# Alternating the two heads of a tile in two attention layers, and padding the tiles that the products read

## The chip, the cores and the metric

The kernel runs on one core of a Trainium2 chip (trn2). The metric is the device time of one launch in microseconds; the median of three runs is quoted. The engines are called as in the profile: PE multiplies matrices (PEld is its loading of weights), DVE, ACT and POOL work on vectors, SP issues most transfers. Every core has a large memory SBUF, which all engines read, and a small one, PSUM, in eight banks of 128 partitions by 512 fp32 numbers, into which PE writes.

## The reference, cut to what matters

Two transformer blocks of two layers each, one after the other, on 512 tokens of width 1024 (the first block puts 16 learned tokens ahead: T = 528). A layer is a mixer and a gated feed-forward network (FFN), each behind a normalization and added to its input. The mixers are: RG-LRU beside sliding-window attention, retention, gated DeltaNet, and attention over three dilated windows. The change touches the two attentions, whose cores are

```python
# first block, layer 0: 8 query heads in 2 groups, one key/value head a group, 64 wide
s = concat([einsum('bnhgqk', q, k_meta), einsum('bnhgqk', q, k_window)]) * 64 ** -0.5   # 16 + 256 keys
s = where(mask, s, NEG_INF)
p = softmax(concat([s, sink]))[..., :-1]
o = p[..., :16] @ v_meta + p[..., 16:] @ v_window
...
# second block, its second mixer: 8 heads of 64, three groups (window, step) = (128, 1), (512, 4), (2048, 16)
logits = where(valid, einsum('brnqhd,brnkhd->brnhqk', q, k) + bias, -inf)   # tokens gathered by step
o_g = einsum('brnhqk,brnkhd->brnqhd', p / l, v);  lse_g = m + log(l)
o = sum_g softmax_g(lse_g) * o_g
```

All is fp32.

## The kernel before, in words

`tile_kernel` (from L1396) runs eight stages, called layers 0 to 7: mixer and FFN in turn. Stages 0 to 2 work on 528 tokens, mostly as two halves of 264; stages 3 to 7 on 512.

**The products.** Every dense product goes through `mm3` (L151). An fp32 number is kept as a high and a low part in PE's faster format fp32r, and each 128x128 block of weights costs three matmuls: high weights by high tokens (L157), high by low (L158), low by high (L159). Such a group is called a triple here. Weights come as 430 transfers of 512 KB and are split on ACT (`whi`, L136) and DVE or POOL (`wlo`, L137). The tokens, PE's moving operand, lie in eight tiles `hhi` and eight `hlo` from `head` (L111), 528 numbers wide whatever the stage, and in `ahi`/`alo` from `act_tile` (L306), as wide as the stage has tokens. Tiles of a name lie one behind the other in SBUF. A tile of 528 numbers takes 2112 bytes, which is 8 x 256 + 64, so its next neighbour begins 64 bytes further on modulo 256; that remainder is called the place of a tile. The eight `hhi` tiles thus go twice through the places 192, 0, 64, 128, in the order in which a product takes them, while `ahi`/`alo` of the stages with 512 tokens (2048 bytes) all have one place, 64. The weights lie at 128.

**The attention of layer 0** (`layer_ab`). `scores(b, kv)` takes a block b of 128 queries and one key/value head kv: four products of 64 rows (the 64 numbers of a head lie on partitions 0 to 63 or 64 to 127), for b > 1 in two pieces of 16 and 256 keys (L565, L566), otherwise in one (L569), then softmax on DVE and ACT. `values(b, kv, s, po)` turns the probabilities round (transposes, L600), copies them out on ACT (L602) and multiplies them with the values (L603), whose result takes 64 of the bank's partitions.

**The attention of layer 6** (`layer_dsw`) goes by four pairs of heads. For each head of the pair: the scores of the undilated group (L1257) and of the two dilated ones (L1266), four to a bank, which DVE takes out of PSUM with scale and bias (`put`, L1249); later the transposes (L1333) and the products with the values (L1349, L1351, and L1363 for the dilated groups). The bias table `tb` of a pair is loaded and the mask added on POOL (L1197).

These products are in plain fp32, and PE does each as two passes, which the profile counts as two matmuls.

**The order** on each engine is set by a scheduler that simulates times and puts first what has priority: the attentions have it, in a strand "b" with its own PSUM banks (4 in layer 0, 3 in layer 6), and the dense products of the same stage fill in between. `aux()` gives the next bank of the strand.

Of the kernel before, what the change touches and what calls it, by code (L numbers as in the profile page):

```python
# [13 lines left out]
OP = mybir.AluOpType  # L14
# [8 lines left out]
HT = T // 2  # L23
NFF = 22
# [27 lines left out]
class Net:  # L52


    def __init__(self, ctx, tc, A):
# [5 lines left out]
        self.hp = ctx.enter_context(tc.tile_pool(name="head", bufs=1))  # L61
        self.hpp = ctx.enter_context(tc.tile_pool(name="headp", bufs=1, space=PSUM))
# [9 lines left out]
    def layer(self, name, acts, width, banks, tmp, pool_split=False):  # L72
# [160 lines left out]
    def rstd(self, sq, n, groups, mul, add):  # L233
# [6 lines left out]
        if G == 2:  # L240
            wide = self.tp.tile([128, 640], F32, name="wide", tag="wide" + self.cur, bufs=2)[:, :m * 64]
            nc.vector.tensor_copy(wide.rearrange("p (g c) -> p g c", c=64), col[:, :, None].to_broadcast([128, m, 64]))
# [62 lines left out]
    def act_tile(self):  # L305
        return (self.ap.tile([128, self.wact], F32R, name="ahi", tag="ahi", bufs=self.nact),  # L306
                self.ap.tile([128, self.wact], F32R, name="alo", tag="alo", bufs=self.nact))
# [133 lines left out]
def layer_ab(N, ctx):  # L441
# [14 lines left out]
    rope = pl.tile([128, 2, T], F32, name="rope")  # L456
# [7 lines left out]
    wa = pl.tile([128, 4, 128], F32, name="wa")  # L464
    nc.gpsimd.dma_start(wa, A["lru_wa"])
    wi = pl.tile([128, 4, 128], F32, name="wi")
# [49 lines left out]

    yah = pl.tile([128, 4, T], F32R, name="yah")
    yal = pl.tile([128, 4, T], F32R, name="yal")

    def attention():  # L520
# [35 lines left out]
        def scores(b, kv):  # L556
# [3 lines left out]
            r = kv * 64  # L560
            s = wk.tile([128, 4, 272], F32, name="s", bufs=3)
            for j in range(4):
                ps = N.aux()
                if b > 1:
                    nc.tensor.matmul(ps[:, 0:16], qkv[r:r + 64, 2 + j, q0:q0 + 128], k[r:r + 64, 0:16], start=True, stop=True)  # L565
                    nc.tensor.matmul(ps[:, 16:nk], qkv[r:r + 64, 2 + j, q0:q0 + 128], k[r:r + 64, q0 - 128:q0 + 128],  # L566
                                     start=True, stop=True)
                else:
                    nc.tensor.matmul(ps[:, :nk], qkv[r:r + 64, 2 + j, q0:q0 + 128], k[r:r + 64, 0:nk], start=True, stop=True)  # L569
                if b == 0:  # L570
# [1035 lines left out]
```

## Time and profile before

| | us |
|---|---|
| three runs | 2919.19, 2932.78, 2938.44 |
| median | 2932.78 |
| profiled execution | 2933.66 |
| its span | 2931.9 |
| PE busy | 2869.4 (98%) |
| DVE busy | 1498.4 (51%) |
| ACT busy | 1027.3 (35%) |
| POOL busy | 404.7 (14%) |

The span is what the profiler saw of the execution, from the first instruction to the last; the 1.8 us around it belong to the launch. Busy time of PE is the union of its matmuls, which overlap: a new one starts before the last has drained. What a matmul costs is therefore read from start to start, not from its duration. The mean clock granted to PE was 0.982 of 2.4 GHz.

### The profile page before, as it was taken

Reading aid. Unit: us, or ns where it says so; the run is one execution under the profiler, and the core shown is the slowest. Engines: PE = TensorE matmul, PEld = TensorE weight load, DVE = VectorE, ACT = ScalarE, POOL = GpSimd, SP = SyncE. Lnnn points to the kernel's source line nnn. Section 1 sums busy time; section 2 is a strip of 40 time slices with the busy share of each in tenths; the row PEclk is TensorE's granted clock in tenths of the full one; section 3 lists DMA queues with packets and bytes.
Section 4 is the critical chain, followed back from the end, with each engine's and each line's share of the span. In section 5 each row is a group of like instructions: output and inputs, shape, how many; then the busy total and the mean of one; then the engine's idle time right before and its main releaser. Section 6 shows DMA issues by size and latency. Waiting matters only on the chain.

```text
span 2931.9 us, 39986 instructions
## 1 busy us (share of the span) xinstructions
PE 2869.4 (98%) x16334; PEld 2455.0 (84%) x16334; DVE 1498.4 (51%) x2553; ACT 1027.3 (35%) x1735; POOL 404.7 (14%) x336
## 2 busy tenths in 40 slices
PE   7899999999999999999999899999999999999999
PEld 7768999998888888888878788888888877888887
DVE  6755953444455368834356854533335575533332
ACT  4634322332222233222266433422224555432221
POOL 3401201100000001001143443100003111000000
PEclk9879999999999999999999899999999999999999
DMA  4102942232212227722222111222222222122222
GB/s 147 54 29 97 340 146 94 94 109 87 72 66 72 87 80 280 258 94 94 91 93 65 58 66 65 94 93 94 94 94 93 75 75 68 51 94 94 95 99 73
DMA packets 93240, 294.79 MB, mean 101 GB/s; under 512 B 18736, under 2 KB 21168, under 8 KB 92928
## 3 DMA queue, kind: packets, MB, share of 16 engines
q1 hardware_dynamic: 91552, 288.59, 28.0%
q8 instruction: 128, 2.10, 0.3%
q10 hardware_dynamic: 1008, 2.22, 0.2%
q0 software_dynamic: 496, 1.43, 0.2%
q14 instruction: 56, 0.46, 0.0%
HBM read 287.42 MB, written 4.26 MB: 99 GB/s over the span
## 4 chain that ended last, share of the span: by engine, by line
PE 92%; DVE 4%; ACT 2%; POOL 1%; issue 1%; DMA 0%; SPq 0%; ACTq 0%; POOLq 0%; DVEq 0%
PE mm L157 26%; PE mm L159 26%; PE mm L158 26%; PE aux L770 1%; PE aux L603 1%; PE aux L227 1%; PE aux L157 1%; PE aux L158 1%; PE aux L159 1%; PE aux L762 1%; PE aux L250 1%; PE aux L1363 1%; PE aux L1333 1%; PE aux L1266 1%; DVE solve L1115 1%
## 5 line engine op out<-in xcount | busy, mean ns | idle before, releaser
L157 PE MATMUL mm<-hhi,whi 128*128 128x512 f32 (+2 forms) x3256 | 1116.3, 345 | 12.2 <-ACT whi L136 10.2
L158 PE MATMUL mm<-hlo,whi 128*128 128x512 f32 (+2 forms) x3256 | 1114.9, 343 | 3.5 <-DVE hlo L122 2.0
L159 PE MATMUL mm<-hhi,wlo 128*128 128x512 f32 (+2 forms) x3256 | 1116.7, 343 | 0.0
L136 ACT ACTIVATE whi<-wraw 128x1024 fp32r<-128x1024 f32 x430 | 455.8, 1061 | 1211.7 <-PE mm L158 849.4
L157 PEld LDWEIGHTS mm<-hhi,whi 128*128 128x128 f32 x3256 | 617.5, 190 | 83.4 <-ACT whi L136 10.2
L158 PEld LDWEIGHTS mm<-hlo,whi 128*128 128x128 f32 x3256 | 619.5, 190 | 76.4 <-DVE hlo L122 2.3
L137 DVE TENSOR_TENSOR wlo<-wraw,whi 128x1024 fp32r<-128x1024 f32 x388 | 485.2, 1251 | 382.4 <-ACT whi L136 381.0
L159 PEld LDWEIGHTS mm<-hhi,wlo 128*128 128x128 f32 x3256 | 619.5, 190 | 71.2 <-issue 0.6
L159 PE MATMUL mm<-ahi,wlo 128*128 128x512 f32 (+2 forms) x1079 | 375.4, 348 | 0.0
L158 PE MATMUL mm<-alo,whi 128*128 128x512 f32 (+2 forms) x1079 | 375.2, 348 | 0.0
L157 PE MATMUL mm<-ahi,whi 128*128 128x512 f32 (+2 forms) x1079 | 374.9, 349 | 0.1
L158 PEld LDWEIGHTS mm<-alo,whi 128*128 128x128 f32 x1079 | 203.2, 188 | 27.9 <-DVE alo L122 0.2
L157 PEld LDWEIGHTS mm<-ahi,whi 128*128 128x128 f32 x1079 | 202.8, 188 | 28.0 <-ACT ahi L121 0.6
L159 PEld LDWEIGHTS mm<-ahi,wlo 128*128 128x128 f32 x1079 | 202.8, 188 | 27.7 <-issue 0.2
L230 POOL TENSOR_TENSOR rcol<-rcol,mhalf 128x4 f32<-128x4 f32 (+4 forms) x46 | 60.0, 1306 | 1187.2 <-DVE rcol L229 1187.1
L388 DVE TENSOR_TENSOR t<-t,mm 128x512 f32<-128x512 f32 (+2 forms) x108 | 61.6, 570 | 210.3 <-PE mm L159 207.2
L380 POOL TENSOR_TENSOR t<-t,acc 128x264 f32<-128x264 f32 (+1 forms) x60 | 80.6, 1345 | 499.5 <-ACT t L379 499.5
L137 POOL TENSOR_TENSOR wlo<-wraw,whi 128x1024 fp32r<-128x1024 f32 x42 | 100.8, 2401 | 189.3 <-ACT whi L136 184.8
L419 DVE SCALAR_TENSOR_TENSOR araw<-araw 128x1024 f32<-128x1024 f32 x96 | 122.8, 1289 | 1.6 <-DMA araw<-in_w_ada 1.4
L432 DVE TENSOR_TENSOR X<-X,mm 128x264 f32<-128x264 f32 (+2 forms) x103 | 54.5, 529 | 115.3 <-PE mm L159 115.2
L121 ACT ACTIVATE ahi<-t 128x512 fp32r<-128x512 f32 (+2 forms) x128 | 69.6, 550 | 83.1 <-DVE t L388 58.3
L434 DVE SCALAR_TENSOR_TENSOR X<-mm,mod,X 128x512 f32<-128x512 f32 (+1 forms) x63 | 43.6, 698 | 93.5 <-PE mm L159 93.1
(459 smaller groups left out, 2739.7 us busy)
## 6 DMA issues: line engine op xcount, KB each, us to landing
wraw<-in_wstream SPq DMA_DIRECT2D x430, 512.0 KB, 3.2
araw<-in_w_ada SPq DMA_DIRECT2D x96, 512.0 KB, 5.3
tb<-in_dsw_bias SPq DMA_DIRECT2D x4, 640.0 KB, 4.6
X<-in_x SPq DMA_DIRECT2D x8, 264.0 KB, 10.8
xd<-X SPq DMA_DIRECT2D x1, 2048.0 KB, 9.1
X<-xd SPq DMA_DIRECT2D x1, 2048.0 KB, 8.5
out_dram<-X SPq DMA_DIRECT2D x4, 512.0 KB, 2.8
dec<-in_c_decay ACTq DMA_DIRECT2D x1, 1056.0 KB, 8.9
```

The costliest lines, as they stand in the source:

```text
L121: self.nc.scalar.activation(hi, src, AF.Copy)
L136: self.nc.scalar.activation(hi, src, AF.Copy)
L137: (self.nc.gpsimd if s < 2 else self.lo_eng).tensor_tensor(lo, src, hi.bitcast(F32), op=OP.subtract)
L157: mm(ps, wh, ah, start=start and k == 0, stop=False)
L158: mm(ps, wh, al, start=False, stop=False)
L159: mm(ps, wl, ah, start=False, stop=stop and k == n - 1)
L230: nc.gpsimd.tensor_tensor(col, col, self.mhalf[:, :m], op=OP.pow)
L380: nc.gpsimd.tensor_tensor(sg, sg, row[:, t0:t0 + n], op=OP.mult)
L388: nc.vector.tensor_mul(sg[:, :n], sg[:, :n], ps)
L419: nc.vector.scalar_tensor_tensor(r, r, 1.0, self.c, op0=OP.mult, op1=OP.mult, accum_out=self.mod[:, m:m + 1])
L432: nc.vector.tensor_add(x, x, ps)
L434: nc.vector.scalar_tensor_tensor(x, ps, gate_col[:, m:m + 1], x, op0=OP.mult, op1=OP.add)
```

## The change

Three things are changed. In layers 0 and 6 the loops are turned inside out: scores of both heads of a tile are issued in turn, each head into a bank of its own, and so are the products with the values, which go to the two halves of one bank. In `head` and `act_tile` tiles of 528 numbers become 576 wide (2304 bytes, 9 x 256), and a tile `pad` of 64 bytes, cleared by POOL, stands ahead of them: all `hhi`, `hlo`, `ahi`, `alo` then lie at place 192, the second half of the 528 tokens at 224. To make room, the mask of layer 6 shrinks (its middle part was a copy of its beginning), so that its add on POOL goes in four pieces a pair instead of one; some tiles of layer 0 share memory with others that are done (`rope`, `wa`, `wi`).

```diff
+TP = 576
...
+            if acts:
+                self.nc.gpsimd.memset(self.ap.tile([128, 16], F32, name="pad"), 0.0)
...
-        return tuple(self.hp.tile([128, T], F32R, name=n, tag=n, bufs=KD)[:, :self.wact] for n in ("hhi", "hlo"))
+        if not self.pad:
+            self.pad = self.hp.tile([128, 16], F32, name="pad")
+            self.nc.gpsimd.memset(self.pad, 0.0)
+        return tuple(self.hp.tile([128, TP], F32R, name=n, tag=n, bufs=KD)[:, :self.wact] for n in ("hhi", "hlo"))
...
+        w = S if self.wact == S else TP
+        return tuple(self.ap.tile([128, w], F32R, name=n, tag=n, bufs=self.nact)[:, :self.wact] for n in ("ahi", "alo"))
...
+    pts = [lambda tag=tag: pl.tile([128, 512], F32, name="pt", tag=tag) for tag in ("wa", "wi", "pt")]
...
+        def scores(b):
...
+            ss.append(pl.tile([128, 4, 272], F32, name="s", tag="rope") if b % 2 else wk.tile([128, 4, 272], F32, name="s", bufs=3))
             for j in range(4):
...
+                pss = [N.aux(), N.aux()]
+                parts = [(0, 16, 0), (16, nk, q0 - 128)] if b > 1 else [(0, nk, 0)]
+                for c0, c1, k0 in parts:
+                    for kv, r in enumerate(rows2):
+                        nc.tensor.matmul(pss[kv][:, c0:c1], qkv[r, 2 + j, q0:q0 + 128], k[r, k0:k0 + c1 - c0],
+                                         start=True, stop=True)
...
+                for s in ss:
+                    pt = N.aux()
+                    for j in range(4):
+                        nc.tensor.transpose(pt[:w, j * 128:j * 128 + 128], s[:, j, c:c + w], N.ident)
+                    p = pts[next(turn) % 3]()
+                    nc.scalar.activation(p[:w], pt[:w], AF.Copy)
+                    ps.append(p)
+                for r, p in zip(rows2, ps):
+                    nc.tensor.matmul(po[r], vt[:w, blk, r], p[:w], start=i == 0, stop=i == len(segs) - 1)
...
-    mask = pl.tile([128, 640], F32, name="dmask")
-    nc.scalar.dma_start(mask, A["c_dsw"])
+    mask = pl.tile([128, 384], F32, name="dmask")
+    nc.scalar.dma_start(mask[:, 0:256], A["c_dsw"][:, 0:256])
+    nc.scalar.dma_start(mask[:, 256:384], A["c_dsw"][:, 512:640])
...
-        nc.gpsimd.tensor_tensor(tb, tb, mask[:, None, :].to_broadcast([128, 2, 640]), op=OP.add)
+        for c0, c1, m0 in ((0, 256, 0), (256, 384, 0), (384, 512, 0), (512, 640, 256)):
+            b = tb[:, :, c0:c1]
+            nc.gpsimd.tensor_tensor(b, b, mask[:, None, m0:m0 + c1 - c0].to_broadcast([128, 2, c1 - c0]), op=OP.add)
...
-            for g in (1, 2):
-                ps = N.aux()
-                for c in range(4):
-                    sl = slice(c * 128, c * 128 + 128)
+        for g in (1, 2):
+            pss = [N.aux(), N.aux()]
+            for c in range(4):
+                sl = slice(c * 128, c * 128 + 128)
+                for r, ps in zip(rows2, pss):
                     nc.tensor.matmul(ps[:, sl], q[r, g, sl], k[r, g, sl], start=True, stop=True)
...
-            p = pl.tile([128, 512], F32, name="dpt", bufs=3)
+            p = pl.tile([128, 512], F32, name="dpt", bufs=4)
...
+        po = [transposed([s0[:, a, sl.stop - 128:sl.stop] for sl in sl0]) for a in range(2)]
+        for b in range(4):
+            d = slice(b * 128, b * 128 + 128)
+            for r, p in zip(rows2, po):
+                nc.tensor.matmul(p0[r, d], v[:, 0, b, r], p[:, d], start=b == 0, stop=False)
...
+        for g in range(2):
+            for a in range(2):
                 nc.vector.tensor_mul(s12[:, a, g], s12[:, a, g], e12[:, g, :, a:a + 1].to_broadcast([128, 4, 128]))
-            pg = [transposed([s12[:, a, g, c] for c in range(4)]) for g in range(2)]
+            pg = [transposed([s12[:, a, g, c] for c in range(4)]) for a in range(2)]
             for c in range(4):
                 d = slice(c * 128, c * 128 + 128)
-                for g in range(2):
-                    nc.tensor.matmul(p12[r, d], v[:, 1 + g, c, r], pg[g][:, d], start=g == 0, stop=g == 1)
+                for r, p in zip(rows2, pg):
+                    nc.tensor.matmul(p12[r, d], v[:, 1 + g, c, r], p[:, d], start=g == 0 and c == 0, stop=g == 1 and c == 3)
```

Lines move down by 8 to 25: the products L157 to L159 become L165 to L167, the scores L565/L566 become L582, L1257 and L1266 become L1276 and L1287, the values L603 becomes L623, L1363 becomes L1388. How PE's order changes is shown at three places; in the rows, a name's number tells tiles of one name apart, and "x4" stands for four alike in a row.

PE in layer 6, the dilated scores of the first pair of heads (`aux` a bank, `dq`/`dk` queries and keys, `mm` a dense product), before:

```order
L157 MATMUL mm_19342<-hhi_18673,whi_19338 128x512
L1266 MATMUL aux_19144<-dk_18775,dq_18774 128x128 x4
L1257 MATMUL aux_19153<-dk_18775,dq_18774 128x128
L1257 MATMUL aux_19153<-dk_18775,dq_18774 128x256
L1257 MATMUL aux_19158<-dk_18775,dq_18774 128x256 x2
L1236 MATMUL aux_19330<-ident_82,t_19328 128x128 x4
```

and now:

```order
L166 MATMUL mm_19319<-hlo_18676,whi_19315 128x512
L1287 MATMUL aux_19161<-dk_18791,dq_18790 128x128
L1287 MATMUL aux_19162<-dk_18791,dq_18790 128x128
L1287 MATMUL aux_19161<-dk_18791,dq_18790 128x128
L1287 MATMUL aux_19162<-dk_18791,dq_18790 128x128
```

Before, four products of one head stand in a row in one bank, then the other head's in other banks; now two banks, one a head, take turns, eight rows of which the first four are shown. Of the 64 dilated scores 40 stand so (the first and third pair of heads, and one group of the fourth); the others stand three or four of a head in a row. Of the 32 undilated ones (L1276) 20 take turns.

PE in layer 6, products of the dilated groups with the values (`dpt` the turned probabilities, `dv` the values; L1333 and L1355 transposes), before:

```order
L208 MATMUL aux_19750<-ident_82,t_19747 128x128 x4
L158 MATMUL mm_19912<-hlo_18674,whi_19908 128x512
L1363 MATMUL aux_19427<-dpt_19435,dv_19257 64x128
L1363 MATMUL aux_19427<-dpt_19442,dv_19257 64x128
L1363 MATMUL aux_19427<-dpt_19435,dv_19257 64x128
```

and now:

```order
L1355 MATMUL aux_21191<-ident_82,s12_20208 128x128 x4
L1388 MATMUL aux_21157<-dpt_21189,dv_20987 64x128
L1355 MATMUL aux_21339<-ident_82,s0_20853 128x128 x4
L1388 MATMUL aux_21157<-dpt_21196,dv_20987 64x128
L1388 MATMUL aux_21157<-dpt_21189,dv_20987 64x128
L1388 MATMUL aux_21157<-dpt_21196,dv_20987 64x128
```

Before, the two tiles `dpt` in turn are two groups of one head, added up in one place; now they are one group of the two heads, which write to the two halves of the bank. Nearly all 120 value products of the layer stand in turn now, though the first of a run of eight often stands some rows ahead, alone, as here.

PE in layer 0, between two blocks of queries (L603 and L623 the values, L600 and L618 transposes of `s`, L565/L566 and L582 scores), before:

```order
L600 MATMUL aux_1401<-ident_82,s_1215 128x128 x4
L600 MATMUL aux_1409<-ident_82,s_1215 128x128 x4
L603 MATMUL aux_1335<-pt_1398,vt_248 64x512
L565 MATMUL aux_1420<-qkv_244 128x16
L566 MATMUL aux_1420<-qkv_244 128x256
L603 MATMUL aux_1335<-pt_1406,vt_248 64x512
L565 MATMUL aux_1424<-qkv_244 128x16
L566 MATMUL aux_1424<-qkv_244 128x256
L603 MATMUL aux_1335<-pt_1414,vt_248 64x512
L565 MATMUL aux_1428<-qkv_244 128x16
L566 MATMUL aux_1428<-qkv_244 128x256
```

and now:

```order
L623 MATMUL aux_1370<-pt_1392,vt_250 64x512
L618 MATMUL aux_1410<-ident_82,s_1172 128x128 x4
L623 MATMUL aux_1370<-pt_1399,vt_250 64x512
L582 MATMUL aux_1423<-qkv_246 128x16
L582 MATMUL aux_1423<-qkv_246 128x256
L623 MATMUL aux_1370<-pt_1408,vt_250 64x512
L582 MATMUL aux_1424<-qkv_246 128x16
L582 MATMUL aux_1424<-qkv_246 128x256
L623 MATMUL aux_1370<-pt_1415,vt_250 64x512
L582 MATMUL aux_1431<-qkv_246 128x16
L582 MATMUL aux_1431<-qkv_246 128x256
```

Before, value products of one head and scores of one head alternate; now each value product has scores or transposes between it and the one of the other head. Of the eleven pairs of value products in the layer three stand side by side. Of the eight pairs of scores with 256 keys four do, of the eight pairs of blocks 0 and 1 (L569) all but a few.

## Rows read from the trace of the kernel before

**Rows 1.** The page, parts 1 and 4: busy engines and the chain that ended last.
```profile
PE 2869.4 (98%) x16334; PEld 2455.0 (84%) x16334; DVE 1498.4 (51%) x2553; ACT 1027.3 (35%) x1735; POOL 404.7 (14%) x336
...
PE 92%; DVE 4%; ACT 2%; POOL 1%; issue 1%; DMA 0%; SPq 0%; ACTq 0%; POOLq 0%; DVEq 0%
PE mm L157 26%; PE mm L159 26%; PE mm L158 26%; PE aux L770 1%; PE aux L603 1%; PE aux L227 1%; PE aux L157 1%; PE aux L158 1%; PE aux L159 1%; PE aux L762 1%; PE aux L250 1%; PE aux L1363 1%; PE aux L1333 1%; PE aux L1266 1%; DVE solve L1115 1%
```

**Rows 2.** Windows: busy us (count) by engine, PEclk, DMA share, GB/s.
```profile
120.00:160.00 40.00, 33.14 (x180) 26.50 (x179) 34.16 (x86) 19.11 (x46) 3.75 (x4) 0.79 0.15 53
185.00:200.00 15.00, 15.00 (x34) 6.23 (x34) 4.13 (x11) 2.17 (x4) 0.00 (x0) 0.50 0.05 19
200.00:215.00 15.00, 14.48 (x38) 7.40 (x37) 6.66 (x21) 6.32 (x22) 0.00 (x0) 0.50 0.00 0
2240.00:2280.00 40.00, 40.00 (x196) 32.06 (x197) 20.52 (x36) 15.66 (x20) 10.48 (x6) 1.00 0.30 105
2280.00:2320.00 40.00, 40.00 (x210) 32.64 (x210) 27.13 (x74) 27.89 (x73) 9.60 (x5) 1.00 0.29 95
```

**Rows 3.** Lines by form, PE: count, busy us, mean ns of one.
```profile
L157 PE MATMUL mm<-hhi,whi 128*128 128x512 f32 x1640 | 652.8, 398 | 0.0
L157 PE MATMUL mm<-ahi,whi 128*128 128x512 f32 x619 | 244.5, 397 | 0.1
L157 PE MATMUL mm<-hhi,whi 128*128 128x264 f32 x1376 | 397.7, 289 | 10.2 <-ACT whi L136 10.2
```

**Rows 4.** Timeline, PE, hhi products from 2821.88 us: start, duration, form.
```profile
2821.88 0.39 PE L157 MATMUL mm<-hhi,whi 128*128 128x512 f32 x1
...
2823.25 0.40 PE L157 MATMUL mm<-hhi,whi 128*128 128x512 f32 x1
...
2824.65 0.39 PE L157 MATMUL mm<-hhi,whi 128*128 128x512 f32 x1
...
2827.42 0.39 PE L157 MATMUL mm<-hhi,whi 128*128 128x512 f32 x1
```

**Rows 5.** Timeline, PE, ahi products from 2874.64 us.
```profile
2874.64 0.40 PE L157 MATMUL mm<-ahi,whi 128*128 128x512 f32 x1
...
2880.24 0.40 PE L157 MATMUL mm<-ahi,whi 128*128 128x512 f32 x1
```

**Rows 6.** Timeline, PE, scores of layer 6, where the head changes.
```profile
2279.93 0.27 PE L1266 MATMUL aux<-dk,dq 64*128 64x128 f32 x1
2280.04 0.27 PE L1257 MATMUL aux<-dk,dq 64*128 64x128 f32 x1
2280.05 0.27 PE L1266 MATMUL aux<-dk,dq 64*128 64x128 f32 x1
2280.15 0.38 PE L1257 MATMUL aux<-dk,dq 64*128 64x256 f32 x1
```

**Rows 7.** Chain of waits, 2230 to 2560 us: shares, then pieces (start, us).
```profile
by line: PE mm L157 21.9%; PE mm L159 21.5%; PE mm L158 21.5%; PE aux L1363 4.9%; PE aux L1333 4.8%; PE aux L1266 4.6%; PE aux L1257 4.1%; PE aux L208 3.4%; PE aux L1349 2.5%; PE aux L227 2.2%; PE aux L1236 1.9%; PE aux L1351 1.9%; PE aux L
...
2285.43 1.98 PE aux L1266 x16
...
2333.47 1.89 PE aux L1363 x16
```

**Rows 8.** Chain of waits, 160 to 245 us.
```profile
by line: PE aux L603 29.5%; PE aux L566 14.8%; PE aux L600 12.2%; PE mm L157 8.2%; PE mm L159 7.9%; PE mm L158 7.8%; PE aux L565 7.1%; ACT pt L602 2.0%; PE aux L157 1.9%; PE aux L158 1.6%; ACT s L582 1.5%; PE aux L159 1.4%; ACT yah L121 1.4
...
180.94 1.00 PE aux L603 x2
...
184.91 1.04 PE aux L566 x2
185.95 1.90 PE aux L603 x2
```

**Rows 9.** Lines: the scores' way out on DVE, the bias table on POOL.
```profile
L1249 DVE SCALAR_TENSOR_TENSOR s<-aux,rq,tb 128x128 f32<-128x128 f32 (+1 forms) x96 | 30.2, 377 | 19.4 <-PE aux L1266 15.4 <-PE aux L1257 3.6
...
L1197 POOL TENSOR_TENSOR tb<-tb,dmask 128x1280 f32<-128x1280 f32 x4 | 11.8, 2942 | 51.6 <-DMA tb<-in_dsw_bias 51.6
```

More of the change, by code (lines that the diff above doesn't have):

```diff
@@ L240, in rstd @@
         if G == 2:
-            wide = self.tp.tile([128, 640], F32, name="wide", tag="wide" + self.cur, bufs=2)[:, :m * 64]
+            wide = self.tp.tile([128, 512 if self.wact == S else 640], F32, name="wide", tag="wide" + self.cur, bufs=2)[:, :m * 64]
             nc.vector.tensor_copy(wide.rearrange("p (g c) -> p g c", c=64), col[:, :, None].to_broadcast([128, m, 64]))
@@ L454, in layer_ab @@
         hs, row = N.take_ahead(H528)
-    rope = pl.tile([128, 2, T], F32, name="rope")
+    rope = pl.tile([128, 2, T], F32, name="rope", tag="rope")
     nc.gpsimd.dma_start(rope, A["c_rope"])
@@ L554, in meta @@
             N.split(yah[:, :, 0:16], yal[:, :, 0:16], pr)
-        def scores(b, kv):
+        rows2 = [slice(kv * 64, kv * 64 + 64) for kv in range(2)]
+        def scores(b):
             q0 = 16 + b * 128
             nk = 144 if b == 0 else 272
-            r = kv * 64
-            s = wk.tile([128, 4, 272], F32, name="s", bufs=3)
+            ss = [wk.tile([128, 4, 272], F32, name="s", bufs=3)]
+            ss.append(pl.tile([128, 4, 272], F32, name="s", tag="rope") if b % 2 else wk.tile([128, 4, 272], F32, name="s", bufs=3))
@@ L562, in scores @@
             for j in range(4):
-                ps = N.aux()
[L564 to L569, printed above, removed]
@@ L570, in scores @@
-                if b == 0:
-                    nc.vector.tensor_scalar(s[:, j, 0:16], ps[:, 0:16], 0.125, None, op0=OP.mult)
-                    nc.vector.scalar_tensor_tensor(s[:, j, 16:144], ps[:, 16:144], 0.125, mask[:, 144:272],
-                                                   op0=OP.mult, op1=OP.add)
-                else:
-                    nc.vector.scalar_tensor_tensor(s[:, j], ps[:, :272], 0.125, mask, op0=OP.mult, op1=OP.add)
-            st = wk.tile([128, 5, 4], F32, name="st")
@@ L593, in values @@
+            return ss
+        def values(b, ss):
             q0 = 16 + b * 128
             nk = 144 if b == 0 else 272
-            r = kv * 64
+            po = N.aux()
             segs = [(0, 16, 0)] + ([(16, 128, b)] if b else []) + [(nk - 128, 128, b + 1)]
             for i, (c, w, blk) in enumerate(segs):
-                pt = N.aux()
-                for j in range(4):
-                    nc.tensor.transpose(pt[:w, j * 128:j * 128 + 128], s[:, j, c:c + w], N.ident)
-                p = wk.tile([128, 512], F32, name="pt", bufs=3)
-                nc.scalar.activation(p[:w], pt[:w], AF.Copy)
-                nc.tensor.matmul(po[r:r + 64], vt[:w, blk, r:r + 64], p[:w], start=i == 0, stop=i == len(segs) - 1)
@@ L617, in attention @@
+                for r, p in zip(rows2, ps):
+                    nc.tensor.matmul(po[r], vt[:w, blk, r], p[:w], start=i == 0, stop=i == len(segs) - 1)
+            N.split(yah[:, :, q0:q0 + 128], yal[:, :, q0:q0 + 128], po.rearrange("p (j q) -> p j q", j=4))
+        ahead = []
+        for b in range(5):
+            if b < 4:
+                ahead.append((b, scores(b)))
+            if b >= 1:
+                values(*ahead.pop(0))
+            if b == 1:
                 meta()
@@ L1337, in transposed @@
             return p
+        rows2 = [slice(64 * a, 64 * a + 64) for a in range(2)]
         p0 = N.aux()
         for a in range(2):
-            r = slice(64 * a, 64 * a + 64)
             for b in range(4):
```

88 lines of the change are left out of this document (41 added, 47 removed).

## The prediction

> **What bounds the kernel now.** I read the page first, for the busy shares and the chain that ended last: PE is busy 98% of the span and carries 92% of the chain, 78% of it in the three matmuls of the triples, every other line 1% or less [rows 1]. So time is won only where PE's own work gets shorter. The windows say where this holds for the two attentions: in layer 6 PE is busy 40.00 of 40 us at a granted clock of 1.00 of 2.4 GHz, while DVE has 20 to 27 [rows 2]; in layer 0, from 185 to 215 us, it is busy 29.48 of 30 at 0.50, the lower level of 1.2 GHz, and has been doing plain fp32 attention products and transposes instead of triples; between 120 and 160 us DVE is as busy as PE, and shorter products there win nothing. The lines by form give the number of triples [rows 3], the timelines what a triple takes by its tile's place [rows 4, 5], and what two row halves of PE do when the head changes [rows 6]; the chains of the two stages give what the attention products cost on the path [rows 7, 8].
>
> **Layer 6, products with the values.** L1363, L1349 and L1351 have 4.9, 2.5 and 1.9% of a chain of 330 us: 30.7 us [rows 7]. Sixteen passes in 1.89 us are 0.118 each. In the new order the two halves of a bank are written in turn. If PE runs the two column halves side by side, a pair takes the time of one. A run of eight whose first stands alone then takes five turns, the pairs that overlap staying one apart, so 3 of 8 is saved: 11.5 us; the smaller runs and their draining leave 10. No row shows two column halves at K = 128 side by side, so the bounds are 0 and 15 (all of it halved); I take 10, since the other way of cutting PE, by rows, does run so (next part). The Trainium skill, "TensorEngine Tiling (Array Packing)", Key Properties, says that different tiles can run matmuls in parallel and lists 128x64 as two tiles; by it the sum stays as it is.
>
> **Layer 6, scores.** L1266 and L1257 have 4.6 and 4.1% of 330 us: 28.7 us. Where the head changes today, a product of the one head starts at 2280.04 and one of the other at 2280.05, and the next step comes at 2280.15 [rows 6]: two passes in the 0.11 us in which one goes alone, against 0.124 in a row of one head (16 in 1.98) [rows 7]. 60 of the 96 products take turns in the new order: 28.7 x 60/96 / 2 = 9.0 us. Four places where the heads meet already overlap, and each group keeps its entry: 7 us. Together 17 at best. Against it stands that a pair takes two of the strand's three banks until DVE has emptied them, eight copies of 30.2/96 = 0.31 us [rows 9], 2.5 us for each of 16 pairs. The next pair stays behind, and PE, in order, with it. Dense triples lie between most of them, and DVE's idle time before these copies is nearly all waiting for PE (19.0 of 19.4 us), so it keeps up; I take off 4 us, a quarter of a microsecond a pair. **Sum of layer 6: -13**, bounds -18 and -4.
>
> **Layer 0.** L603 and L566 have 29.5 and 14.8% of 85 us, 25.1 and 12.6 us [rows 8]. Three of the eleven pairs of value products stand side by side: each saves one product, 1.00 us at the full clock, 1.90 at the half: 3 to 5.7. Four of eight pairs of scores do: one product of 256 keys, 0.5 to 1.04 each: 2 to 4. The others have a transpose or a score of 128 rows between them, which takes the whole array. The scores of blocks 0 and 1 fall in the stretch that DVE bounds: nothing. **-7**, between -5 and -10 with the order as it is; what the clock may add is a rival below.
>
> **Padding.** The eight `hhi` tiles take turns by place: two triples at 192 and 0 take 2823.25 - 2821.88 = 1.37 us, two at 64 and 128 take 1.40, and eight take 5.54, so 0.685, 0.70 and a mean of 0.6925 [rows 4]. A stream with all its tiles at 64 takes 5.60 for eight, 0.700 [rows 5]. The place therefore matters by about 2% in some streams. All at 192: if each triple keeps 0.686, 1640 x 0.0065 = 10.7 us from `hhi` and 619 x 0.014 = 8.7 from `ahi`, 19 in all. But one place for all was a little worse than the same place in turn in the stream that shows it (0.700 against 0.70, some 2 ns by finer reading than these rows give); and no stream has all at 192. I take -2 ns for `hhi` (3 us) and -8 ns for `ahi` (5 us): **-8**, bounds -19 and +3 (the 264-wide products, 1376 triples and more, whose halves go to 192 and 224, may lose as much as 2 ns each). The Trainium skill, "SBUF — State Buffer", section "Who interferes with whom", gives PE two independent read ports and says that PE never waits on anyone; by it nothing would depend on the place, and the term would be 0. The measured 0.685 against 0.70 speaks against that.
>
> **What I cost at nothing.** The add on POOL, 2.94 us four times, becomes four pieces each; nobody is seen waiting for it, and POOL is busy 9.6 to 10.5 of 40 us there [rows 2, 9]. Without that cover it would be a microsecond or two a pair. The `pad` memsets are tiny and stand at a stage's start on POOL; they come before tiles that are filled only after the previous stage's last products, so they wait for what the norm waits for anyway. The second DMA for the mask is on ACT's queue, long before its use. Tiles of layer 0 in the place of `rope`, `wa` and `wi` wait for the rotary and the gates, which are done before the attention's products. The scheduler also shuffles layer 4, whose code is as before: 0, with 5 us either way.
>
> **The sum.** -13 - 7 - 8 = -28: 2933.66 - 28 = 2905.7, so **2905 us**. The profiled execution lies 0.9 us above the median of 2932.78, so nothing is corrected for.
>
> **The rivals.** About 1% (29 us) is what a measurement of this kernel can tell from no change: its runs lie between 2919 and 2938.
> - *The place of a tile costs nothing once they are all alike.* For it: the only stream with one place is the slowest seen [rows 5]. Against: 192 is the quick place in turn [rows 4]. -20: 2913. The page on SBUF would lead here too.
> - *All of it comes.* Every pair overlaps without a wait, padding gives its bound: -17 - 8 - 19 = -44: 2889. Or PE, with more at once, keeps the full clock in layer 0: 30 us at 0.50 would shrink by up to 15, of which half gives 2898 with the rest as forecast. For it: the clock came back to 1.00 later in the same stage; against: triples are rare there in the new order too, and these are the products with which it fell.
> - *Column halves don't run side by side*, so the change does only half of what it says: without 10 in layer 6 and 4 in layer 0, -14: 2919. For it: no row shows it; against: rows halves do.
> - *PE waits for banks.* In layer 6 each of 16 pairs of scores waits until DVE has emptied both banks of the pair before, 2.5 us: +40 - 28 = +12: 2945, slower than before. It decides from 1.75 us a pair on (28/16). For it: three banks, two a pair, PE in order. Against: DVE waits for PE there and not the other way [rows 9], and triples stand between.
>
> **Chances.** Forecast 0.45, place worth nothing 0.17, all of it 0.2, no column halves 0.12, banks 0.06. The range goes from 2885, which takes in nearly all of the full gain, to 2928, which holds the third rival with its 5 us for layer 4; the bank case and the tails of the others stay out. Over 1% faster means below 2903.5: the case with all of it, half of the forecast's, little else: 0.45. Slower by over 1% (above 2962) would need the bank case with the padding's bad end: 0.02. The rest, 0.53, lies within 1%.
>
> **What would show it.** In the changed kernel's profile: in layer 6, L1287's and L1388's passes starting in twos, sixteen in about 1 us instead of 1.98 and 1.89, and both lines' shares of the chain halved. Eight triples of `hhi` in 5.49 to 5.54 us and of `ahi` in 5.50 to 5.56; if `ahi` stays at 5.60, the padding term is wrong. No new line of PE's waits above a few us; if L1276, L1287 or L1388 wait there for DVE or ACT, the bank rival holds. Passes of L1388 that start one after the other 0.11 us apart show that column halves don't overlap. A granted clock above 0.50 between 185 and 215 us would put the time near 2890.

## The result, and the profile after

The changed kernel takes 2889.02 us (median of four runs, 2887.19 to 2891.03), against 2929.91 for the kernel before: a ratio of 0.9862, 95% interval 0.9828 to 0.9897. Forecast were 2905 us and a range of 2885 to 2928. The time lies in the range, 16 us under the forecast.

The kernel before has two times, since the granted clock in layer 0 differs from run to run (the trace of e3, below, shows it). In 58 later runs beside the experiments 20 took 2917 to 2921 us, 29 took 2932 to 2936, and 9 lay between. The profiled execution of before, on which the prediction rests, is of the longer kind. So -41 by the medians is -29 against the shorter time and -44 against the longer.

The page of the changed kernel, busy time and chain:

```profile
span 2887.7 us, 40005 instructions
...
PE 2821.9 (98%) x16334; PEld 2430.6 (84%) x16334; DVE 1490.7 (52%) x2553; ACT 1026.7 (36%) x1735; POOL 408.0 (14%) x355
...
PE 90%; DVE 4%; ACT 3%; issue 1%; POOL 1%; DMA 0%; SPq 0%; ACTq 0%; POOLq 0%; DVEq 0%
```

PE is the bound as before [rows 1]: its busy time fell by 47.5 us, the span by 44.2. DVE, ACT and POOL are where they were.

Where the time came from is read from the starts of the 430 splits of weights (`whi`, L136 before, L144 now): the same split stands before the same product in every version, so the difference of its start, taken at the edges of the stages, is what each stage gained. "After" is the changed kernel, the other columns are the experiments below; every number is the stage's change in us against the profiled execution before.

| stage | after | e1 padding | e2 layer 0 | e3 layer 6 | e4 no padding | e8 halves | e9 place 128 |
|---|---|---|---|---|---|---|---|
| layer 0 | -16.9 | +1.5 | -19.4 | -14.5 | -19.2 | -24.2 | -26.5 |
| layers 1, 2 | -0.1 | 0.0 | 0.0 | 0.0 | 0.0 | 0.0 | -5.8 |
| layer 3 (FFN, 512) | -4.5 | -4.5 | 0.0 | 0.0 | 0.0 | -5.6 | -6.8 |
| layer 4 | +0.5 | +0.7 | +1.7 | -0.2 | +1.6 | -0.2 | +0.1 |
| layer 5 (FFN, 512) | -4.7 | -4.2 | 0.0 | 0.0 | 0.0 | -4.2 | -7.0 |
| layer 6, norm behind it | -14.2 | -0.2 | -0.5 | -11.0 | -12.7 | -14.1 | -18.0 |
| rest of layer 7 (FFN) | -3.5 | -3.5 | 0.0 | 0.0 | 0.0 | -3.5 | -6.2 |
| sum | -43.3 | -10.2 | -18.2 | -25.8 | -30.3 | -51.7 | -70.2 |

Note e3: its layer 0 is the old one, and yet 14.5 us shorter. That is the other clock: its layer 0 has 20.5 us at the lower level of 1.2 GHz, the profiled execution before has 51.2. The layer 0 of "after" and e2 has 20.5 us too, so they compare with e3 at one clock.

**Layer 0.** The windows of the changed kernel over the stretch of [rows 2]:

```profile
185.00:200.00 15.00, 13.25 (x69) 7.01 (x68) 7.24 (x18) 5.87 (x16) 0.00 (x0) 1.00 0.11 35
200.00:215.00 15.00, 13.49 (x49) 4.79 (x48) 6.23 (x22) 8.41 (x27) 0.00 (x0) 0.89 0.00 1
```

Both stood at 0.50 before; now the granted clock is 1.00 and 0.89 (a mean over the window of the two levels, 1.00 and 0.50).

What the order did at one clock is read from the chain of waits from 160 to 245 us. In e3, with the old layer 0:

```profile
by line: PE aux L603 22.3%; PE aux L566 10.0%; PE mm L157 9.7%; PE aux L600 9.7%; PE mm L159 9.3%; PE mm L158 9.3%; PE aux L157 5.7%; PE aux L158 5.4%; PE aux L159 5.3%; PE aux L565 5.2%; ACT pt L602 2.0%; ACT s L582 1.5%; ACT yah L121 1.4%
```

and in the changed kernel:

```profile
by line: PE aux L623 18.5%; PE mm L165 11.3%; PE aux L582 10.5%; PE mm L166 9.5%; PE mm L167 9.3%; PE aux L618 7.8%; ACT s L598 6.9%; PE aux L165 6.0%; PE aux L167 5.8%; PE aux L166 5.7%; ACT pt L620 3.4%; PE aux L235 1.4%; issue 1.3%; ACT 
```

Of 85 us, the value products (L603, now L623) fell by 3.2 us and the scores (L565 and L566, now L582) by 4.0. But the softmax on ACT (L582 before, L598 now) rose from 1.3 to 5.9 us of the chain, and the copies of the turned probabilities (`pt`) from 1.7 to 2.9: with PE faster, this stretch waits for ACT in part.

**Layer 6.** The chain of waits from 2215 to 2530 us, pieces (start, us):

```profile
2244.30 1.09 PE aux L1287 x16
...
2307.33 1.02 PE aux L1388 x16
...
2506.11 9.18 PE aux L235 x44
```

and of the kernel before, from 2230 to 2560 us, the same sums of the norm:

```profile
2549.32 5.48 PE aux L227 x44
```

Sixteen passes of the dilated scores take 1.09 us instead of 1.98, sixteen of the value products 1.02 instead of 1.89 [rows 7]: row halves and column halves both run side by side. By the trace the sixteen starts come in twos, at most 0.01 us apart, and mostly 0.11 us from one two to the next; before, the value products started one at a time, 0.11 us apart. Taken from each start to PE's next, all attention products of the layer cost 42.0 us instead of 60.7: the value products 20.2 instead of 30.4, the scores 21.9 instead of 30.3. None of their lines is among PE's waits. But the layer became only 14.2 us shorter, and these rows say where most of the rest went: 44 sums of the norm behind it take 9.18 us (L235), where they took 5.48 before (L227). The granted clock is lower there. The windows over the layer's end, of the changed kernel,

```profile
2505.00:2515.00 10.00, 10.00 (x52) 10.00 (x52) 2.04 (x4) 1.98 (x4) 0.70 (x1) 0.53 0.15 52
2515.00:2525.00 10.00, 9.50 (x65) 8.77 (x65) 7.05 (x15) 5.61 (x15) 3.68 (x6) 0.78 0.00 0
```

and of the kernel before:

```profile
2540.00:2550.00 10.00, 9.85 (x70) 8.66 (x68) 8.86 (x16) 6.99 (x13) 0.00 (x0) 1.00 0.16 55
2550.00:2560.00 10.00, 9.50 (x57) 8.78 (x58) 5.29 (x11) 3.53 (x10) 2.81 (x4) 0.66 0.16 52
2560.00:2570.00 10.00, 9.81 (x83) 9.61 (x82) 6.19 (x14) 8.26 (x19) 4.57 (x6) 1.00 0.01 2
```

The stretch with a reduced clock grew at the layer's end: 0.53 and 0.78 over 20 us, where the kernel before has 0.66 over 10 us and 1.00 on either side.

**Padding.** Starts of `hhi` products (eight triples apart) and of `ahi` products in the last FFN, timeline of PE:

```profile
2775.95 0.39 PE L165 MATMUL mm<-hhi,whi 128*128 128x512 f32 x1
...
2781.44 0.39 PE L165 MATMUL mm<-hhi,whi 128*128 128x512 f32 x1
...
2830.20 0.39 PE L165 MATMUL mm<-ahi,whi 128*128 128x512 f32 x1
...
2835.69 0.39 PE L165 MATMUL mm<-ahi,whi 128*128 128x512 f32 x1
```

2781.44 - 2775.95 = 5.49 us for eight triples of `hhi` and 2835.69 - 2830.20 = 5.49 for `ahi`, where it was 5.54 and 5.60 [rows 4, 5].

### The profile page after: what moved, and what is told of

Same layout as the page of the kernel before. It is cut to its first block, busy times and chain, and to the rows that moved or that the text cites. A ratio compares the mean times of both kernels' runs of the same rounds, so it can differ in the third digit from the quotient of the medians.

```text
span 2887.7 us, 40005 instructions
## 1 busy us (share of the span) xinstructions
PE 2821.9 (98%) x16334; PEld 2430.6 (84%) x16334; DVE 1490.7 (52%) x2553; ACT 1026.7 (36%) x1735; POOL 408.0 (14%) x355
## 3 DMA queue, kind: packets, MB, share of 16 engines
q1 hardware_dynamic: 91552, 288.59, 28.8%
## 4 chain that ended last, share of the span: by engine, by line
PE 90%; DVE 4%; ACT 3%; issue 1%; POOL 1%; DMA 0%; SPq 0%; ACTq 0%; POOLq 0%; DVEq 0%
PE mm L165 26%; PE mm L167 26%; PE mm L166 26%; PE aux L786 1%; PE aux L235 1%; DVE solve L1131 1%; PE aux L778 1%; PE aux L165 1%; PE aux L166 1%; PE aux L167 1%; PE aux L623 1%; PE aux L1355 1%; PE aux L258 1%; PE aux L216 0%; ACT whi L144 0%
## 5 line engine op out<-in xcount | busy, mean ns | idle before, releaser
L165 PE MATMUL mm<-hhi,whi 128*128 128x512 f32 (+2 forms) x3256 | 1115.8, 344 | 17.8 <-ACT whi L144 9.8
L167 PE MATMUL mm<-hhi,wlo 128*128 128x512 f32 (+2 forms) x3256 | 1114.6, 343 | 0.0
L144 ACT ACTIVATE whi<-wraw 128x1024 fp32r<-128x1024 f32 x430 | 455.1, 1059 | 1207.6 <-PE mm L166 843.9
L165 PEld LDWEIGHTS mm<-hhi,whi 128*128 128x128 f32 x3256 | 618.0, 191 | 87.5 <-ACT whi L144 9.8
L167 PEld LDWEIGHTS mm<-hhi,wlo 128*128 128x128 f32 x3256 | 619.9, 190 | 68.6 <-issue 1.0
L167 PE MATMUL mm<-ahi,wlo 128*128 128x512 f32 (+2 forms) x1079 | 373.6, 346 | 0.0
L165 PE MATMUL mm<-ahi,whi 128*128 128x512 f32 (+2 forms) x1079 | 372.3, 346 | 0.2 <-DVE X L442 0.2
L166 PEld LDWEIGHTS mm<-alo,whi 128*128 128x128 f32 x1079 | 202.7, 188 | 26.1 <-issue 0.2
L167 PEld LDWEIGHTS mm<-ahi,wlo 128*128 128x128 f32 x1079 | 202.7, 188 | 25.8 <-issue 0.3
L165 PEld LDWEIGHTS mm<-ahi,whi 128*128 128x128 f32 x1079 | 202.6, 188 | 24.8 <-DVE X L442 0.4
```

What stands on the lines that cost most here:

```text
L144: self.nc.scalar.activation(hi, src, AF.Copy)
L165: mm(ps, wh, ah, start=start and k == 0, stop=False)
L166: mm(ps, wh, al, start=False, stop=False)
L167: mm(ps, wl, ah, start=False, stop=stop and k == n - 1)
```

## The experiments

**e1, padding alone.** The edit: `head`, `act_tile`, the pads and the smaller mask as in the change; both attentions in the old order. For room, the turned probabilities of layer 0 use the memory of `wa` and `wi`:

```diff
-                p = wk.tile([128, 512], F32, name="pt", bufs=3)
+                p = pts[next(turn) % 3]()
```

> The padding alone (and the smaller mask; the turned probabilities of layer 0 use the shared memory), both attentions in the old order. Theory: the padding is worth what the trace of the changed kernel shows by place, so the three FFNs with 512 tokens shrink by about 4 us each, the 264-wide stages by nothing: -12 to -16 us, about 2917; layer 0 keeps its stretch at clock 0.50. Rival 1, the place costs nothing and the change's gain is all in the attentions: within 4 us of before. Rival 2, the padding (or the shared memory) is what keeps the clock up in layer 0: -25 to -30 us, about 2902.

Measured: 2913.65 us median, 0.9961 [0.9937, 0.9986]; five runs near 2907, five from 2919 to 2924. The trace has the three FFNs 4.5, 4.2 and 3.5 us shorter, the other stages as before: -11.7 behind layer 0. The profiled run has the old clock in layer 0:

```profile
185.00:200.00 15.00, 14.46 (x35) 6.49 (x34) 4.64 (x12) 2.98 (x8) 0.00 (x0) 0.53 0.10 35
200.00:215.00 15.00, 14.48 (x36) 7.00 (x35) 6.80 (x23) 6.71 (x22) 0.00 (x0) 0.50 0.00 0
```

So the padding is worth 12 us, in the 512-wide triples alone, and does not keep the clock up: rival 2 falls. So does rival 1: the shorter runs went from 2918 to 2907 and the longer from some 2933 to 2923. The shared memory for the turned probabilities is in this kernel too, and half of its runs are of the longer kind.

**e2, layer 0 alone** (`layer_ab` as changed, all else as before).

> The head alternation of layer 0 alone. Theory: -17 us, all of it between 160 and 245 us, some 10 of it because the granted clock stays near 1.00 there; about 2913. Rival, the clock stayed up for another reason than the order: the stretch at 0.50 is back and only -5 to -7 us is left, about 2924.

Measured: 2915.32 us, 0.9973 [0.9955, 0.9992], ten runs between 2914.5 and 2922.4. The trace gives -19.4 in layer 0. Against the longer time of before that is the -17 of the expectation and 2 more, clock included; against the shorter (e3's -14.5) it is -4.9.

**e3, layer 6 alone** (`layer_dsw` as changed, all else as before).

> The head alternation of layer 6 alone, with its four-piece mask add. Theory: layer 6 shrinks by 12 to 14 us (the value products' chain from 31 to about 20 us, the scores' from 29 to about 21), about 2917. Rival, the shrinking of layer 6 came mostly from the padding of its dense products: 5 us or less, about 2925.

Measured: 2922.82 us, 0.9987 [0.9965, 1.0009]: by the total nothing, since nine of its ten runs lie from 2920 to 2924 at a mean granted clock of 0.98, while half of those of before beside them are of the shorter kind. The trace settles it: layer 6 is 11.0 us shorter, one less than the 12 to 14 expected, though its attention products cost 42.8 us, nearly what they cost in the changed kernel; the clock behind the layer is at the lower level for 17 us, against 7 in the kernel before. The longer runs agree, 2923 against 2933. And the profiled run is the tenth, 2907.8 us, with the unchanged layer 0 at the full clock:

```profile
185.00:200.00 15.00, 14.05 (x58) 6.65 (x59) 8.21 (x22) 5.93 (x17) 0.00 (x0) 1.00 0.10 35
200.00:215.00 15.00, 14.51 (x71) 7.78 (x70) 7.77 (x26) 8.61 (x26) 0.00 (x0) 1.00 0.00 1
```

PE's order in layer 0 is row for row that of the kernel before, at 1.00 instead of 0.50 [rows 2]. This row is what shows that the 14.5 us belong to the clock and not to the order.

**e4, both alternations, no padding.**

> Both alternations without the padding. Theory: the terms add up, so -30 us, about 2900, and the FFNs with 512 tokens are as long as before. Rival, the parts overlap (padding and order move the same waits): the sum of the three parts differs from the whole change by more than 10 us.

Measured: 2902.66 us, 0.9925 [0.9898, 0.9953]; FFNs as before. At the clock of e3's layer 0 the parts add up: -4.9 (e2) - 11.0 (e3) = -15.9, measured -30.3 + 14.5 = -15.8; with e1's -11.7 it is -27.6, and the whole change has -43.3 + 14.5 = -28.8. (e1's layer 0, +1.5, is left out of this sum, since its clock is another; with it the sum is -26.1. The rival's 10 us are not reached either way.)

**e5, another place.** The pads made 192 bytes long:

```diff
-            self.pad = self.hp.tile([128, 16], F32, name="pad")
+            self.pad = self.hp.tile([128, 48], F32, name="pad")
```

> The changed kernel with pads of 192 bytes instead of 64, so that all token tiles lie at place 64 instead of 192. Theory: the place itself sets a triple's time, so the 512-wide triples go back to about 0.700 us as in the one stream that had all its tiles at 64: some 13 ns on about 2000 triples, +26 us on the changed kernel, about 2915. Rival: what helps is that all tiles lie at one place, whichever it is: as the changed kernel, 2889 within 4 us.

Measured: 2895.4 us (two runs), 0.9898 [0.9847, 0.9949]. Here the edit did not do what its expectation says: `ahi` and `alo` lie behind both pads and so stayed at 192 (192 + 192 bytes is 64 + 64 modulo 256); only `hhi` and `hlo` went to 64. Those did what the theory said. `hhi` products in the last FFN, eight triples apart:

```profile
2781.94 0.40 PE L165 MATMUL mm<-hhi,whi 128*128 128x512 f32 x1
...
2787.54 0.40 PE L165 MATMUL mm<-hhi,whi 128*128 128x512 f32 x1
```

2787.54 - 2781.94 = 5.60 us, 0.700 a triple; the mean over all 1361 undivided triples is 0.6998, with `ahi` at 192 still 0.687. So not "one place for all" helps but the place. The total rose by 6 us against the changed kernel and not by the 26 expected, since `ahi` did not move and layers 0 to 2 gained 9 us. A surprise came with it: in the retention layer, which reads its 512 tokens 64 bytes further on, the same tiles lie at 128, where the weights lie, and its 178 triples took 0.6815, less than any stream before.

**e6, layer 0 by head.** Layer 0's new loop over blocks with its four score tiles, but no alternation: scores and value products of one head, then the other's.

```diff
-                pss = [N.aux(), N.aux()]
-                for c0, c1, k0 in parts:
-                    for kv, r in enumerate(rows2):
-                        nc.tensor.matmul(pss[kv][:, c0:c1], qkv[r, 2 + j, q0:q0 + 128], k[r, k0:k0 + c1 - c0],
+            for kv, (r, s) in enumerate(zip(rows2, ss)):
+                for j in range(4):
+                    ps = N.aux()
+                    for c0, c1, k0 in parts:
+                        nc.tensor.matmul(ps[:, c0:c1], qkv[r, 2 + j, q0:q0 + 128], k[r, k0:k0 + c1 - c0],
...
```

> Layer 0 alone changed, with the new loop over blocks and the new shared memory but scores and value products by head as before (layer 6 and the tiles as before). Theory: it is the turning of the heads that keeps the granted clock up in layer 0, so without it the runs fall again on two times some 15 us apart, about 2918 and 2933, as those of the kernel before do. Rival: the new loop over blocks does it, and all runs lie near 2915.

Measured: 2919.23 us, 0.9972 [0.9953, 0.999]; ten runs from 2913.7 to 2924.1, none near 2933. My theory fell. The windows:

```profile
185.00:200.00 15.00, 15.00 (x66) 7.81 (x64) 5.40 (x13) 3.57 (x6) 0.00 (x0) 0.89 0.09 35
200.00:215.00 15.00, 13.07 (x49) 5.62 (x50) 6.27 (x22) 9.27 (x28) 0.00 (x0) 0.89 0.00 1
```

The clock dips for a few microseconds in each window and recovers, without any alternation.

**e7, layer 0, scores alone in turn** (e2 with the value products by head, as in e6).

> Layer 0 alone changed, scores in turn, value products by head. Theory: the value products of 512 columns are the longest of the stretch and decide the clock, so some runs are again 15 us longer, the others near 2917. Rival: the scores in turn are enough, all runs near 2916.

Measured: 2917.63 us, 0.9967 [0.9948, 0.9986]; ten runs from 2915.9 to 2920.8. No longer runs here, so the theory fell. By the medians the alternation of layer 0 is worth 2919.2 - 2915.3 = 3.9 us (e6 against e2), of which the scores have 1.6; by the profiled layer 0 it is 5.2 us (-14.2 in e6, -14.8 in e7, -19.4 in e2), of which the scores have 0.6. Part of this is clock, since layer 0 has 27 us at the lower level in e6's profile, 24 in e7's and 20 in e2's. How it divides is not shown.

**e8, halves.** On the changed kernel: a bank of transposes in layer 0 holds two query heads of each of the two key/value heads, so one copy feeds two value products, one a head, that are ready together:

```diff
-                ps = []
-                for s in ss:
-                    pt = N.aux()
-                    for j in range(4):
-                        nc.tensor.transpose(pt[:w, j * 128:j * 128 + 128], s[:, j, c:c + w], N.ident)
+                for h in range(2):
+                    pt = N.aux()
+                    for kv, s in enumerate(ss):
+                        for j in range(2):
+                            at = kv * 256 + j * 128
+                            nc.tensor.transpose(pt[:w, at:at + 128], s[:, 2 * h + j, c:c + w], N.ident)
...
+                    for kv, r in enumerate(rows2):
+                        nc.tensor.matmul(po[r, h * 256:h * 256 + 256], vt[:w, blk, r], p[:w, kv * 256:kv * 256 + 256],
```

> The changed kernel, in which a bank of transposes in layer 0 now holds two columns of queries of both heads instead of four of one, so that one copy feeds two value products of 256 columns, one a head, which always stand side by side (eleven pairs became twenty-two, of half the size; before only three of eleven did). Theory: column halves run side by side, so eight of the eleven pairs save one product of 512 columns, about 0.85 us each, where PE is the bound: -4 to -7 us on the changed kernel, 2883 to 2885. Rival: the stretch waits for ACT by now, and nothing is gained, 2889; or the smaller products pay for more switches between forms, up to +4 us.

Measured: 2882.76 us (2881.12 to 2885.92), 0.9856 [0.9823, 0.9889]: 6.3 us under the changed kernel. (e5 and e8 to e10 ran beside the kernel before and not beside the changed one; the shortest runs of before lie between 2917.2 and 2919.2 in the different sets, so 2 us of such a difference may be due to that. By the starts it is 8.4.) Its chain of waits has the pairs,

```profile
204.16 0.59 PE aux L619 x4
204.74 0.58 PE aux L623 x4
205.33 0.54 PE aux L619 x4
...
208.96 0.58 PE aux L623 x4
209.53 0.59 PE aux L619 x4
210.12 0.58 PE aux L623 x4
```

and the changed kernel's has, for the same products:

```profile
200.67 0.59 PE aux L618 x4
201.26 1.00 PE aux L623 x2
202.25 0.60 PE aux L618 x4
```

Four passes, a product of 256 columns of each head, take 0.58 us; two passes of one head's 512 columns took 1.00, so the pair of heads 2.00 where now two such fours take 1.16.

**e9, halves at the weights' place.** e8 without the head pool's pad, which puts the tiles at 128:

```diff
-            self.pad = self.hp.tile([128, 16], F32, name="pad")
-            self.nc.gpsimd.memset(self.pad, 0.0)
```

> The run with halves, and all token tiles at place 128, where the weights lie, by leaving out the head pool's pad (second halves of 528 tokens at 160; the 512-wide products of the retention layer at 192). Theory: in the run at place 64 the retention layer's products happened to lie at 128 and took 0.6815 us a triple against 0.687 at 192; so some 2000 triples of 512 win 5.5 ns, and the retention layer's 178 win 11: -11 to -13 us on the run with halves, about 2870. Rival: 0.6815 belongs to that layer and not to the place; within 3 us of 2883.

Measured: 2862.54 us (2862.25 to 2865.45), 0.9771 [0.9747, 0.9795]: the best of the study, 26 us under the changed kernel. `hhi` products in the last FFN, eight triples apart:

```profile
2761.71 0.39 PE L162 MATMUL mm<-hhi,whi 128*128 128x512 f32 x1
...
2767.15 0.39 PE L162 MATMUL mm<-hhi,whi 128*128 128x512 f32 x1
```

5.44 us, 0.680 a triple. That is 20 us under e8, where 11 to 13 were expected: the stages with 512 tokens gained what was forecast, and the halves of 264 tokens gained as well (layers 1 and 2: -5.8, of which some 2 were expected; layer 0: 2.3 beyond e8).

**e10, the weights moved instead.** The changed kernel, a pad of 64 bytes ahead of the weights in place of the one ahead of `hhi`: weights at 192, tokens at 192 as in the change.

```diff
+        self.nc.gpsimd.memset(self.wp.tile([128, 16], F32, name="pad"), 0.0)
```

> The changed kernel with the weights moved by 64 bytes, from place 128 to 192, and the token tiles left at 192. Theory A, what counts is where the tokens lie against the weights: a 512-wide triple with both at one place takes 0.6815 us, as with both at 128; total about 2880. Theory B, the tokens' own place counts: 0.687, total 2889.

Measured: 2871.5 us (two runs), 0.9799 [0.9768, 0.983], 17.5 under the changed kernel. The same eight triples:

```profile
2762.08 0.39 PE L163 MATMUL mm<-hhi,whi 128*128 128x512 f32 x1
...
2767.52 0.39 PE L163 MATMUL mm<-hhi,whi 128*128 128x512 f32 x1
```

5.44 us again, the tokens at the place where the change had 5.49. The total fell by more than the 9 us of theory A, as in e9: layers 1 and 2 have -5.7 here too. Theory A holds for the triple: what counts is where the tokens lie against the weights. A rival, which neither theory names, is that the tokens' place and the weights' place each have a price of their own, and 192 is simply a good place for weights. The retention layer tells them apart, since it reads its tokens 64 bytes further on, at place 0. Eight triples of it in the changed kernel, with the weights at 128:

```profile
740.08 0.39 PE L165 MATMUL mm<-hhi,whi 128*128 128x512 f32 x1
...
745.65 0.40 PE L165 MATMUL mm<-hhi,whi 128*128 128x512 f32 x1
```

and the same eight in e10, with the weights at 192:

```profile
733.37 0.39 PE L163 MATMUL mm<-hhi,whi 128*128 128x512 f32 x1
...
738.86 0.39 PE L163 MATMUL mm<-hhi,whi 128*128 128x512 f32 x1
```

5.57 us became 5.49: 0.696 and 0.686 a triple (means over the layer: 0.698 and 0.689). With a price for the weights' place alone these triples would have gained what the others did, 0.006; they gained 0.009, down to about the 0.687 of the other streams that lie 64 bytes beyond the weights.

**e11, the old loop with a fourth score tile.**

```diff
-            s = wk.tile([128, 4, 272], F32, name="s", bufs=3)
+            s = pl.tile([128, 4, 272], F32, name="s", tag="rope") if b % 2 and kv else wk.tile([128, 4, 272], F32, name="s", bufs=3)
```

> The kernel before with one thing of layer 0's change: a fourth tile for the scores (in the memory of the rotary table), the loop by block and head as before. Theory: with three tiles a block's second head waited for the first's to come free, which bunched the long plain products; with the fourth the runs with 15 us more are gone and all lie near 2918. Rival: the loop's order does it; about half of the runs lie near 2933 still.

Measured: 2916.65 us, 0.9963 [0.9945, 0.9982]; eight runs from 2914 to 2919.5, two at 2930.6 and 2932.0. Inconclusive: the tile left the order on PE, DVE and ACT as it was, so this is in effect the kernel before again, and two long runs of ten against half of 58 are too few to say whether the tile itself helps. The long runs are still there, so the expectation that all lie near 2918 fell.

## Why the prediction held, step by step

- **Layer 6, -13 (bounds -18 and -4): measured -14.2.** The mechanism was right: both halves of PE run side by side, for the columns too, which no row had shown. The Trainium skill, "TensorEngine Tiling (Array Packing)", says under Key Properties that tiles work in parallel and lists 128x64 as two tiles under Available Configurations; this case's rows agree (1.02 us for sixteen passes). The value products gained 10.2 us (10 forecast) and the scores 8.4 (7 forecast), 18.7 together. The bank waits for which I took off 4 did not come. What took back 4 to 5 us is a longer stretch of reduced clock behind the layer, in the norm's sums (+3.7), of which no step of the prediction spoke. That the sum is only 1 us off is luck in that much: a wait that was feared stayed away, and a cost that was not thought of took its place.
- **Layer 0, -7: measured -16.9, of which -14.5 is the clock.** At one clock the layer gained 2.4 (the change against e3) to 4.9 (e2 against e3): the term was too large. Part of the difference between the two goes with the padding (e4 without it has -19.2, the change -16.9); how is not shown. The products themselves gave about what was forecast, 7.2 us of the chain. The step that failed is that only PE's products were costed: ACT's softmax and copies, 3.0 us of the chain in e3, take 8.8 now, and no term of the sum has them. Besides, a score does not take the whole array, as the prediction says of it: its form is 64*128 [rows 6].
- **The clock in layer 0.** The rival "keeps the full clock" came true, and at its price: "up to 15". Its reason was wrong: I put it on PE doing more at once, but e6 has no longer runs either, with no alternation. What the runs show is that the new loop over blocks goes with it: of 51 runs of kernels with the new loop none is more than 10.4 us above its kernel's shortest; of the 88 with the old loop (before, e1, e3, e11) 45 lie 12 us or more above it.
- **Padding, -8 (bounds -19 and +3): measured -11.7 (e1).** Right in sign, too small. The step that failed is "one place for all was a little worse than the same place in turn": at 192 it was a little better (0.6869 against 0.688). I had it from the one stream that lay at 64. The row was read as a property of having one place; it was a property of that place, measured from the weights (e10). The order of the places is also given wrongly ahead of the prediction and in it: a product takes its tiles in the order 128, 64, 0, 192, by the addresses in the program, so the row at 2821.88 is a tile at 0 and the next one at 192; the quick pair and the slow pair are as the prediction has them. The Trainium skill, "SBUF — State Buffer", section "Who interferes with whom", by which PE's two reads are independent and the term would be 0, is contradicted by e10: 0.680 against 0.687 us for the same tokens, when only the weights move.
- **Nothing for the rest: measured.** The add on POOL, the memsets and the second DMA show nowhere; layer 4, reshuffled, has +0.5.
- **The sum.** -28 was forecast; at equal clock it is 2918 - 2889 = -29. The terms did not all hold: layer 0 gave less than forecast, the padding more (-12.7 in the three FFNs of the change), and the two errors cancel. The step that failed for the total is "nothing is corrected for": the remaining 15 us, which make the profiled runs differ by 44, are the clock in layer 0 of the profiled execution, of the longer kind. The three runs given (2919, 2933, 2938) held the warning: one lay 14 us from the next. And that 2889 is also the price of the rival "all of it comes" is chance: neither its padding (-19) nor its layer 6 (-17) was measured; the clock made up the difference.

## What to carry to other kernels

Where two heads share a tile and PE is the bound, issue their small products in turn, rows or columns, and make both ready by one copy: in the changed kernel a value product that was parted from its pair took 1.00 us, in e8 a pair of products of half the columns took 0.58 together. Then see which engine the stretch waits for next. For 512 columns, lay the moving operand at the same place modulo 256 bytes as the weights (other widths must be tried, see below), and look at a stage by its own starts, since the total of a run can hide 11 us (e3) behind a clock that changes by itself. Before a single profiled execution is the base of a sum, compare its clock by stage with that of another run. A stream that is slow in one layout says something about that layout, not about all that are uniform.

## What the runs showed of the hardware that I had not expected

The time of a 512-wide triple depends on where the tokens lie against the weights, modulo 256 bytes. Means over all undisturbed triples whose neighbours lie at the same place, at full clock:

| tokens minus weights | us a triple | triples | run |
|---|---|---|---|
| 0 | 0.6815 | 1368 | e9 (0.6814 in e10) |
| 64 | 0.6869 | 1368 | after |
| 128 | 0.6978 | 178 | after, retention layer |
| 192 | 0.6998 | 1361 | e5 |

In the FFNs alone the first row is 0.680, as the rows of e9 and e10 have it. The table holds for tiles that all lie at one place. In turn, as in the kernel before, the mean of eight triples (5.54/8 = 0.6925) is near the mean of the table, 0.6915, but [rows 4] have the tiles at 64 and 128 as the slow pair, and 128 is the quickest place alone; which tile a delay belongs to isn't told by the starts.

Products of 264 columns follow another rule (`hhi`): 0.3614 us at 0 and 0.3652 at 32 (e9), 0.3626 at 64 and 0.371 at 96 (after), 0.3639 at 192 and 0.3609 at 224 (e5). Products of 256 columns are slowest where those of 512 are quickest: 0.360 with tokens and weights at one place (e9, e10), 0.340 to 0.353 in the changed kernel and e5. Eight such triples in the changed kernel and the same eight in e9:

```profile
1080.80 0.28 PE L165 MATMUL mm<-hhi,whi 128*128 128x256 f32 x1
...
1083.52 0.28 PE L165 MATMUL mm<-hhi,whi 128*128 128x256 f32 x1
```

```profile
1065.85 0.28 PE L162 MATMUL mm<-hhi,whi 128*128 128x256 f32 x1
...
1068.73 0.28 PE L162 MATMUL mm<-hhi,whi 128*128 128x256 f32 x1
```

2.72 us against 2.88. Why, is open.

The second thing is the clock in layer 0: one order of PE, with 30 us at 0.50 in the profiled execution before and at 1.00 in e3's. From 150 to 180 us, ahead of the stretch, PE is busy 30.00 of 30 us at 1.00 in both; in it, it does mostly plain fp32 products and transposes. What decides in a run is not settled, nor what in the new loop prevents it: alternation is not needed for it (e6), the shared memory of the turned probabilities is not enough (e1), and with the fourth score tile alone long runs are left (e11). The order by whole blocks and the place of the dense products among them were not tried apart.
